# Decoding the fourth token block with the other three in a hybrid SSD, attention and PEER layer

## Chip, cores and metric

One core of one Trainium2 chip runs the whole layer in one launch. The metric is the device time in microseconds of one execution; the figure for the kernel before is the median of three runs. The profile is of one further execution, so its own time stands beside its span below.

## What is computed

512 tokens of width 1024 pass a layer norm, a mixer (16 SSD heads and 8 latent-attention heads, one output projection) and a PEER expert layer. Only the PEER part matters here:

```python
s = einsum('thkd,hknd->thkn', q, sub_keys)          # 8 heads, 2 halves, 128 keys each
sv, si = top_k(s, 16)                               # per half
cand_s = sv[:, :, 0, :, None] + sv[:, :, 1, None, :]
top_s, top_pos = top_k(cand_s.reshape(..., 256), 16)
expert_idx = take_along_axis(cand_i, top_pos)       # one of 16384 experts
gate = softmax(top_s)
act = gelu(x . u_table[expert_idx])                 # 128 experts a token
out = sum(gate * act * v_table[expert_idx])
```

The result then goes through a last residual layer norm.

## The kernel before, in words

**Two ways to do PEER.** The 512 tokens are four blocks of 128. Blocks 0 to 2 (384 tokens) are done densely: the expert tables are cut into 128 chunks of 128 experts, a *U chunk* multiplies one chunk of `u_table` with the tokens (24 matmuls of 336 columns, then GELU on ScalarE, L1416), and a *V chunk* multiplies gated activations with one chunk of `v_table` (18 matmuls of 512 columns, L1680 to L1684). The last 48 tokens of block 2 are left out of the U matmuls and gather their `u_table` rows instead (`ug_fetch`, `ug_dots`). Block 3 is done wholly by gathers: 128 rows a token of `u_table`, then 128 of `v_table` (`gather`, L1540; `fetch`, L1558): POOL issues an indirect DMA of 512 KB for one expert of each of the 128 tokens, and VectorE multiplies (L1572) or accumulates (L1578) it.

**Weights.** Each chunk comes by a 512 KB load on SP's queue (`wir`, L105), is rounded on ScalarE (`wih`, L123), and its low part is made on VectorE (`wil`, L133). Loads, roundings and splits run two chunks ahead of TensorE.

**Order of the work.** Every engine runs its instructions in the order of the program. The order is a plan made by Python generators: a `yield` names the VectorE time that a step is thought to take, and `drive` (L1482) adds half a U chunk to the program whenever the planned TensorE time (3.75 us a chunk, `T_U`) is not ahead of the planned VectorE time. A U chunk charges 1.2 us of VectorE too. The stages from the scores on are:

1. query projection and top 16 of blocks 0 to 3 (`stage1`);
2. `stage2` (L1111): `decode` of blocks 0 to 2, which turns positions into expert numbers by one-hot products (L1093 to L1103) and scores into gates; U chunks between;
3. `build_g` (L1228), the *gate build*: dense gate tiles for blocks 0 to 2 by f16 matmuls, 48 steps. Every fourth step fills a staging tile `stg` of 16 KB a partition, from the pools `gs0` and `gs1` in turn; ScalarE's queue stores it to `gsp` in DRAM in three pieces (L1310), and of the last two staging tiles a small part goes to `gs0` in DRAM (L1306). The last tile (number 11) lies in pool `gs0`. U chunks run between, up to `AHEAD`, later up to `PRE - RES`;
4. `late3` (L1116): block 3's scores and positions, which were parked in DRAM (`t3d`), are loaded again on POOL's queue and decoded alone, beside the U chunks up to number `PRE - 1`;
5. the V stage: `load_g` (L1604) loads gate tiles `gt`, for the first two groups of four chunks on POOL's queue (L1610); `v_prep` (L1630) multiplies activations and gates, `v_hi` and `v_lo` split the product `P` into `Ph` and `Pl`. `GAP` V chunks run alone, then U and V chunks in turn until U's 128 are done, then V alone. Block 3's gathers are spread over the remaining units of work (L1727 to L1731). Each `fetch` keeps four rows in flight.

Activations stay in SBUF for `KEEP` chunks; the next ones are parked in DRAM (`asp`) until the pools `act2` and `act3` open, and come back on POOL's queue (L1411). Of the first chunks (`done`, up to 40) the gates are multiplied in place during the gate build (L1316).

**Pools.** SBUF pools are stacks. `gp2` (rows of the gather, `hd`, `ac`) opens on the right side; in that order on the same side lie `xt`, then `ijp`, then `gs1`, `gs0` and `gb` while the gate build runs. A tile framework adds the waits: the first access in a new pool waits for what the closed pools that it overlaps still have under way, stores included.

The lines of the start of the V stage, in their order:

```python
fill = gather()
next(fill)                       # L1599
...
for q in range(2):
    load_g(q)                    # L1617
refill()
```

Of the kernel before, what the change touches and what calls it, by code (L numbers as in the profile page):

```python
# [11 lines left out]
F32 = mybir.dt.float32  # L12
F32R = mybir.dt.float32r
F16 = mybir.dt.float16
# [21 lines left out]
NA = ND * 32 + 32  # L36
PIECES = 3
FIRST = 40
KEEP = 51
MORE = 12  # L40
REST = 5
LEAD = KEEP + MORE + REST
PRE = 74
AHEAD = 68
GAP = max(0, PRE - LEAD - 1)
UROWS = 4
RES = 3
# [20 lines left out]
def tile_block(ctx: ExitStack, tc: tile.TileContext, I, out):  # L68
# [6 lines left out]
    def pool(name, bufs=1, **kw):  # L75
        p = tc.alloc_tile_pool(name=name, bufs=bufs, **kw)
        opened.append(p)
        return p
# [868 lines left out]
    spare = lambda c0: XT[:, :, c0:c0 + 64].bitcast(F32)  # L947
    wide = lambda z: z.rearrange("p (a b) -> p a b", b=64)
    scl = xt.tile([128, 1], F32, name="scl")
    xt.tile([128, 64], F32, name="edge")  # L950
    one16 = xt.tile([128, NA - NU], F32, name="one16")
    V.memset(one16, 1.0)
# [93 lines left out]
            cand, h = late_c.pop()  # L1046
            yield (0.7 if m == 15 else 0.0) + top16(cand, 88, TS4[:, :, h], PO4[:, :, h])

    t3d = [dram.tile([128, n, 16], dt, name=nm) for n, dt, nm in ((8, F32, "ts3"), (8, U32, "po3"), (16, U32, "ti3"))]

    def decode(p, TS, PO, TI, ia, blocks, nb):
        f4 = lambda z: z.rearrange("p b h k -> p (b h k)")
        g4 = lambda z: z.rearrange("p b h k -> p (b h) k")
        d = p.tile([128, nb, 8, 16], F32, name="dd")
        V.tensor_tensor(g4(d), g4(TS), g4(TS)[:, :, 0:1].to_broadcast([128, nb * 8, 16]), op=OP.subtract)
        sm_ = lambda n, dt=F32: p.tile([128, nb * 128], dt, name=n)
        p3, p2, pf, b1 = sm_("p3", U32), sm_("p2", U32), sm_("pf"), sm_("b1")
        a1, af, sm = p3.bitcast(F32), p2.bitcast(F32), b1[:, :nb * 8]
        abf = p.tile([128, nb, 2, 128], F16, name="abf")
        ti = p.tile([128, 2, 8, 16, 2], F16, name="tif", bufs=min(nb, 2))  # L1060
        pos = f4(PO)
        ab = lambda e: abf[:, :, e]
        v4 = lambda z: z.rearrange("p (b k) -> p b k", b=nb)
        V.tensor_scalar(p3, pos, 3, None, op0=OP.logical_shift_right)
        V.tensor_scalar(p2, pos, 2, None, op0=OP.logical_shift_right)
        V.tensor_copy(pf, pos)
        yield 1.2 if nb > 1 else 0.6
        V.tensor_scalar(a1, p3, -1.0, 0.0, op0=OP.add, op1=OP.max)
        V.scalar_tensor_tensor(af, p2, -6.0, a1, op0=OP.add, op1=OP.max)
        V.tensor_scalar(a1, af, 8.0, 8.0, op0=OP.mult, op1=OP.add)  # L1070
        V.tensor_scalar(b1, af, 4.0, 24.0, op0=OP.mult, op1=OP.add)
        yield 1.3 if nb > 1 else 0.7
        V.tensor_copy(ab(0), v4(af))
        V.tensor_tensor(a1, a1, b1, op=OP.min)
        V.tensor_scalar(b1, af, 0.0, 8.0, op0=OP.is_equal, op1=OP.mult)
        V.tensor_tensor(pf, pf, a1, op=OP.subtract)
        V.tensor_tensor(ab(1), v4(pf), v4(b1), op=OP.add)
        yield 2.0 if nb > 1 else 1.0
        A.activation(f4(d), f4(d), AF.Exp)
        V.tensor_reduce(sm, g4(d), axis=AX.X, op=OP.add)  # L1080
        V.reciprocal(sm, sm)
        for b in range(nb):
            o = IJG[blocks[b]] = (ijp if nb > 1 else p).tile([128, 3, 8, 16], F32, name="ijg", bufs=nb)
            V.tensor_tensor(o[:, 2], d[:, b], sm[:, b * 8:(b + 1) * 8, None].to_broadcast([128, 8, 16]), op=OP.mult)
        yield 1.6 if nb > 1 else 0.8
        sh = [128, 16, 16, 16]
        for b in ((2, 0, 1) if nb > 1 else (0,)):
            for c in range(2):
                A.activation(ti[:, :, :, :, c].rearrange("p e h a -> p h e a"),
                             TI[:, b].rearrange("p (h e) a -> p h e a", e=2), AF.Copy)  # L1090
            eq = p.tile([128, 16, 16, 16], F16, name="eq")
            abv = abf[:, b].rearrange("p e (h k) -> p (e h) k", k=16)
            V.tensor_tensor(eq, abv[:, :, None, :].to_broadcast(sh), ia[:, None].to_broadcast(sh), op=OP.is_equal)  # L1093
            yield 2.3
            eqv = eq.rearrange("p g a (k c) -> p (g a) k c", c=2)
            tv = ti.rearrange("p e h a c -> p (e h a) c")
            V.tensor_tensor(eqv, eqv, tv[:, :, None, :].to_broadcast([128, 256, 8, 2]), op=OP.mult)
            if nb > 1 and b != 1:
                ti = p.tile([128, 2, 8, 16, 2], F16, name="tif", bufs=2)
            yield 2.3  # L1100
            for w in (8, 4, 2):
                V.tensor_tensor(eq[:, :, :w], eq[:, :, :w], eq[:, :, w:2 * w], op=OP.add)
            V.tensor_tensor(IJG[blocks[b]][:, 0:2].rearrange("p e h k -> p (e h) k"), eq[:, :, 0], eq[:, :, 1], op=OP.add)  # L1103
            yield 2.8
            if nb > 1 and b == 2:
                ug_index(p3)
            if nb > 1 and b == 1:
                yield next(UR["dots"])
                g_head(0)

    def stage2():  # L1111
        yield from decode(rt2, TS4[:, :3], PO4[:, :3], TI4[:, :3], iaE, (0, 1, 2), 3)

    late = []

    def late3():  # L1116
        lt = pool("lt", side="right")
        t = [lt.tile([128, 1, n, 16], dt, name=nm) for n, dt, nm in ((8, F32, "ts"), (8, U32, "po"), (16, U32, "ti"))]
        ia = lt.tile([128, 16, 16], F16, name="iaE")
        G.dma_start(ia.rearrange("p a b -> p (a b)"), I["ch"][:, 256:512])  # L1120
        for z, src in zip(t, t3d):
            G.dma_start(z[:, 0], src)
        yield 3.4
        yield from decode(lt, *t, ia, (3,), 1)
        late.append(lt)

    GT, UR = {}, {}
    done = []
# [1 line left out]
    def ug_index(tmp):  # L1130
        ijg = IJG[2]
        f = lambda z: z.rearrange("p h k -> p (h k)")
        ix = tmp[:, :128].bitcast(I32)
        V.scalar_tensor_tensor(ix, f(ijg[:, 0]), 128.0, f(ijg[:, 1]), op0=OP.mult, op1=OP.add)
        G.dma_start(ugi, ix[128 - UG:])
        G.dma_start(ugg, f(ijg[128 - UG:, 2]))
        for k, dst in spread(ugi, UR["ix"]):
            G.dma_start(dst, k)
        G.dma_start(UR["g"], ugg)
        for n in range(UROWS):  # L1140
            ug_fetch(n)
        for dst, t in zip(t3d, (TS4, PO4, TI4)):
            G.dma_start(dst, t[:, 3])
        UR["dots"] = ug_dots()

    def spread(d, t):
# [81 lines left out]
    def build_g():  # L1228
# [44 lines left out]
        for n in range(48):  # L1273
# [24 lines left out]
            if g % 4 == 3:  # L1298
                k = n // 4
                if k < ND:  # L1300
                    done.append(min(FIRST, (un[0] - 2) // 4 * 4))
                    late.append((n + 2, k, stg))
                    e = [done[k] + (128 - done[k]) * x // PIECES for x in range(PIECES + 1)]
                    stores.extend((gsp[k][:, x:y], stg[:, x:y]) for x, y in zip(e, e[1:]))
                else:
                    nc.scalar.dma_start(gs0[:, :, k - ND], stg[:, 0:8].rearrange("j (q i) t -> j q (i t)", q=2))  # L1306
                    e = [8 + 120 * x // PIECES for x in range(PIECES + 1)]
                    stores.extend((gsp[k][:, x:y], stg[:, x:y]) for x, y in zip(e, e[1:]))
# [229 lines left out]
    GS = [-1, 0, 0]  # L1538

    def gather():  # L1540
        yield from late3()
        ijg = IJG.pop(3)
        ix = gp_.tile([128, 128], I32, name="ix")
        f = lambda z: z.rearrange("p h k -> p (h k)")
        V.scalar_tensor_tensor(ix, f(ijg[:, 0]), 128.0, f(ijg[:, 1]), op0=OP.mult, op1=OP.add)
        g3 = gp_.tile([128, 128], F32, name="g3")
        V.tensor_copy(g3, f(ijg[:, 2]))
        close(*late, ijp)
        yield 0.5
        gp2 = pool("gp2", side="right")  # L1550
        x3 = UR["x3"]
        hd = gp2.tile([128, 128], F32, name="hd")
# [5 lines left out]
        def fetch(s):  # L1558
            if s < 256:
                R[s] = gp2.tile([128, D], F32, name="row", bufs=ROWS)  # L1560
                G.indirect_dma_start(out=R[s], out_offset=None, in_=I["u"] if s < 128 else I["v"],  # L1561
                                     in_offset=bass.IndirectOffsetOnAxis(ap=ix[:, s % 128:s % 128 + 1], axis=0))
        for s in range(ROWS - 1):
            fetch(s)
        for s in range(256):
# [26 lines left out]

    aps.append(pool("act3"))
    edge = pool("edge")
    edge.tile([128, 64], F32, name="edge")
    vst = pool("vst")
    gp_ = pool("gp")
    fill = gather()
    next(fill)  # L1599
    gt = {}  # L1600

# [97 lines left out]
    for c in range(2):  # L1699
        while uc < PRE - 1 + c:  # L1700
            u_chunk(uc)
            uc += 1
            if GS[0] < 0:
                pump(fill, 2.6)
        v_hi(c, v_prep(c))
        v_lo()
    more = True
# [175 lines left out]
```

## Time and profile before

| | |
|---|---|
| runs | 1572.33, 1577.47, 1578.97 us (median 1577.47) |
| profiled execution, its own time | 1574.32 us |
| its span | 1572.6 us |
| granted TensorE clock, mean | 0.998 |
| TensorE busy | 1546.8 us (98%) |
| VectorE busy | 1346.1 us (86%) |
| ScalarE busy | 767.9 us (49%) |
| POOL busy | 622.8 us (40%) |
| DMA, mean | 259 GB/s |

Busy shares are means over stages with different limits. A busy TensorE is not TensorE at its peak, since the ends of matmuls are modelled; the times from one matmul's start to the next say more.

### The profile page before, as it was taken

The page shows a single profiled execution, that of the slowest core. Times are in us where ns is not written, and L with a number is a line of the kernel's source. Part 1 is how long each engine was busy: PE and PEld are TensorE (multiplying, and loading weights), DVE is VectorE, ACT ScalarE, POOL GpSimd, SP SyncE. Part 2 cuts the span into 40 slices and gives each one's busy share as a digit, 9 for nine tenths or more (in the row PEclk, how much of TensorE's full clock was granted, in tenths as well). Part 3 has the DMA queues.
Part 4 walks back from the last instruction along what each step waited for, and adds up shares of the span by engine and source line. Part 5 has one row for each costly group of instructions (what it writes and reads, how often), then busy time and mean ns, then how long its engine had stood idle before and what let it go on. Part 6 is the DMA issues. An engine that isn't in the chain of part 4 may idle for free.

```text
span 1572.6 us, 24526 instructions
## 1 busy us (share of the span) xinstructions
PE 1546.8 (98%) x8696; PEld 1358.0 (86%) x8696; DVE 1346.1 (86%) x2643; ACT 767.9 (49%) x1539; POOL 622.8 (40%) x455
## 2 busy tenths in 40 slices
PE   9999999999999999999999999999999999999997
PEld 7887888888888999999998999999988878888886
DVE  8979767747799989999976888888889889899997
ACT  5565467741433547777755444444433344434442
POOL 0010032510134534443114666565555557667610
PEclk9999999999999999999999999999999999999999
DMA  6242122474323568999779999999989999999983
GB/s 253 94 161 83 55 78 54 128 244 148 124 88 101 137 226 291 358 336 326 271 251 335 351 361 358 350 359 386 373 320 371 360 366 372 357 359 364 370 280 141
DMA packets 150171, 406.53 MB, mean 259 GB/s; under 512 B 14280, under 2 KB 55448, under 8 KB 149792
## 3 DMA queue, kind: packets, MB, share of 16 engines
q1 hardware_dynamic: 94080, 208.11, 38.9%
q0 software_dynamic: 50096, 177.12, 31.0%
q10 hardware_dynamic: 5872, 19.73, 3.1%
q8 instruction: 68, 1.11, 0.3%
q14 instruction: 55, 0.45, 0.1%
HBM read 374.16 MB, written 28.65 MB: 256 GB/s over the span
## 4 chain that ended last, share of the span: by engine, by line
PE 75%; DVE 10%; DMA 7%; issue 4%; ACT 3%; POOL 1%; DVEq 0%; ACTq 0%; POOLq 0%
PE va L1684 9%; PE va L1681 9%; PE va L1680 9%; PE pu L86 8%; PE pu L88 8%; PE pu L87 8%; DMA wir<-v 4%; PE pa L87 3%; PE pa L86 3%; PE pa L88 3%; PE pw L87 3%; PE pw L88 3%; PE pw L86 3%; DVE wil L133 2%; DMA wir<-ut 2%
## 5 line engine op out<-in xcount | busy, mean ns | idle before, releaser
L123 ACT ACTIVATE wih<-wir 128x1024 fp32r<-128x1024 f32 (+2 forms) x269 | 277.7, 1033 | 259.4 <-DMA wir<-v 161.2
L133 DVE TENSOR_TENSOR wil<-wir,wih 128x1024 fp32r<-128x1024 f32 (+1 forms) x234 | 282.9, 1212 | 80.5 <-ACT wih L123 55.1
L88 PE MATMUL pu<-XT,wil 128*128 128x336 f32 x1008 | 319.2, 317 | 5.4 <-DVE wil L133 5.3
L1681 PE MATMUL va<-wil,Ph 128*128 128x512 f32 x726 | 283.0, 390 | 0.0
L1561 POOL DMA_INDIRECT row<-v,ix x128 | 217.5, 1699 | 136.6 <-DVE ac L1578 114.7
L1680 PE MATMUL va<-wih,Ph 128*128 128x512 f32 x624 | 243.5, 390 | 0.0
L1561 POOL DMA_INDIRECT row<-u,ix x128 | 186.8, 1460 | 132.6 <-DVE row L1572 96.6
L86 PE MATMUL pu<-XT,wih 128*128 128x336 f32 x648 | 207.5, 320 | 0.0
L87 PE MATMUL pu<-XT,wih 128*128 128x336 f32 x648 | 204.5, 316 | 0.0
L88 PEld LDWEIGHTS pu<-XT,wil 128*128 128x128 f32 x1008 | 189.3, 188 | 8.0 <-DVE wil L133 8.0
L1684 PE MATMUL va<-wih,Pl 128*128 128x512 f32 x624 | 193.2, 391 | 1.4 <-DVE Pl L1671 1.3
L1578 DVE SCALAR_TENSOR_TENSOR ac<-row,hd,ac 128x1024 f32<-128x1024 f32 x128 | 164.1, 1282 | 8.5 <-DMA row<-v,ix 6.8
L1681 PEld LDWEIGHTS va<-wil,Ph 128*128 128x128 f32 x726 | 136.4, 188 | 26.6
L1572 DVE SCALAR_TENSOR_TENSOR row<-row,XT 128x1024 f32<-128x1024 f32 x128 | 150.8, 1222 | 9.7 <-DMA row<-u,ix 9.6
L1684 PEld LDWEIGHTS va<-wih,Pl 128*128 128x128 f32 x624 | 116.9, 188 | 27.3 <-DVE Pl L1671 2.7
L1680 PEld LDWEIGHTS va<-wih,Ph 128*128 128x128 f32 x624 | 117.2, 188 | 22.7
L133 POOL TENSOR_TENSOR wil<-wir,wih 128x1024 fp32r<-128x1024 f32 (+3 forms) x35 | 72.9, 2093 | 154.5 <-PE pw L88 99.4
L87 PEld LDWEIGHTS pu<-XT,wih 128*128 128x128 f32 x648 | 121.9, 188 | 1.1
L86 PEld LDWEIGHTS pu<-XT,wih 128*128 128x128 f32 x648 | 121.7, 188 | 1.2
L1155 POOL DMA_INDIRECT urow<-u,uix x48 | 74.1, 1543 | 107.2 <-DVE urow L1161 98.8
L123 ACT ACTIVATE wihx<-wir 128x1024 fp32r<-128x1024 f32 x67 | 70.9, 1058 | 91.8 <-DMA wir<-ut 55.6
L1663 ACT ACTIVATE Ph<-P 128x384 fp32r<-128x384 f32 x121 | 62.7, 518 | 107.5 <-DVE P L1640 90.2
(520 smaller groups left out, 3389.9 us busy)
## 6 DMA issues: line engine op xcount, KB each, us to landing
wir<-ut SPq DMA_DIRECT2D x128, 512.0 KB, 6.1
wir<-v SPq DMA_DIRECT2D x128, 512.0 KB, 6.7
gt<-gsp SPq DMA_DIRECT2D x22, 768.0 KB, 10.2
wir<-wo SPq DMA_DIRECT2D x26, 512.0 KB, 3.7
wir<-wf SPq DMA_DIRECT2D x18, 512.0 KB, 3.3
wir<-wqr SPq DMA_DIRECT2D x16, 512.0 KB, 3.5
gsp<-stg ACTq DMA_DIRECT2D x12, 464.0 KB, 6.4
de<-acd POOLq DMA_DIRECT2D x8, 512.0 KB, 5.4
```

The costliest lines, as they stand in the source:

```text
L86: T.matmul(ps, lh, rh, start=start, stop=False)
L87: T.matmul(ps, lh, rl, start=False, stop=False)
L88: T.matmul(ps, ll, rh, start=False, stop=stop)
L123: A.activation(h, r, AF.Copy)
L133: self.lo(n).tensor_tensor(l, r, h, op=OP.subtract)
L1155: G.indirect_dma_start(out=UR[n], out_offset=None, in_=I["u"], in_offset=bass.IndirectOffsetOnAxis(ap=UR["ix"][:, n:n + 1], axis=0))
L1561: G.indirect_dma_start(out=R[s], out_offset=None, in_=I["u"] if s < 128 else I["v"], in_offset=bass.IndirectOffsetOnAxis(ap=ix[:, s % 128: ...
L1572: V.scalar_tensor_tensor(wide(r), wide(r), 1.0, x3, op0=OP.mult, op1=OP.mult, accum_out=hd[:, s:s + 1])
L1578: V.scalar_tensor_tensor(ac, r, hd[:, s - 128:s - 127], ac, op0=OP.mult, op1=OP.add)
L1680: T.matmul(va[b][e], Ph[b], h[:, cs], start=c == 0, stop=False)
L1681: T.matmul(va[b][e], Ph[b], l[:, cs], start=False, stop=False)
L1684: T.matmul(va[b][e], Pl[b], h[:, cs], start=False, stop=c == 127)
```

## The change

Block 3 is decoded in `stage2` with the other three, after block 1 and the first gate tile's head; its expert numbers `ix3` and gates `g3` are kept in `xt`. `late3`, the parking in `t3d` and the loads back are gone. `gather()` is advanced twice ahead of the first `load_g`, so that its four first fetches stand there in POOL's program. `PRE` goes from 74 to 72, so V chunk 0 comes after 72 U chunks; `AHEAD` goes from 68 to 70, `KEEP` from 51 to 50, and `GAP`, worked out from them, from 5 to 4. The planner is charged more for the decode. `done` no longer lags two chunks behind.

```diff
-KEEP = 51
+KEEP = 50
...
-PRE = 74
-AHEAD = 68
+PRE = 72
+AHEAD = 70
...
     scl = xt.tile([128, 1], F32, name="scl")
+    ix3 = xt.tile([128, 128], I32, name="ix3")
+    g3 = xt.tile([128, 128], F32, name="g3")
...
-        yield 1.2 if nb > 1 else 0.6
+        yield 1.5
...
-        yield 1.3 if nb > 1 else 0.7
+        yield 1.6
...
-        yield 2.0 if nb > 1 else 1.0
+        yield 2.5
...
-            o = IJG[blocks[b]] = (ijp if nb > 1 else p).tile([128, 3, 8, 16], F32, name="ijg", bufs=nb)
+            o = IJG[blocks[b]] = ijp.tile([128, 3, 8, 16], F32, name="ijg", bufs=3) if b < 3 else p.tile([128, 3, 8, 16], F32, name="ijg3")
...
-        yield 1.6 if nb > 1 else 0.8
+        yield 2.1
...
-        for b in ((2, 0, 1) if nb > 1 else (0,)):
+        for b in (2, 0, 1, 3):
...
-            if nb > 1 and b == 1:
+            if b == 1:
                 yield next(UR["dots"])
                 g_head(0)
+            if b == 3:
+                ijg = IJG.pop(3)
+                f = lambda z: z.rearrange("p h k -> p (h k)")
+                V.scalar_tensor_tensor(ix3, f(ijg[:, 0]), 128.0, f(ijg[:, 1]), op0=OP.mult, op1=OP.add)
+                V.tensor_copy(g3, f(ijg[:, 2]))
+                yield 0.5
 
     def stage2():
-        yield from decode(rt2, TS4[:, :3], PO4[:, :3], TI4[:, :3], iaE, (0, 1, 2), 3)
-
-    late = []
-
-    def late3():
...
+        yield from decode(rt2, TS4, PO4, TI4, iaE, (0, 1, 2, 3), 4)
...
-        for dst, t in zip(t3d, (TS4, PO4, TI4)):
-            G.dma_start(dst, t[:, 3])
         UR["dots"] = ug_dots()
...
-                    done.append(min(FIRST, (un[0] - 2) // 4 * 4))
+                    done.append(min(FIRST, un[0] // 4 * 4))
...
     def gather():
-        yield from late3()
...
-        close(*late, ijp)
-        yield 0.5
+        close(ijp)
         gp2 = pool("gp2", side="right")
...
     edge = pool("edge")
-    edge.tile([128, 64], F32, name="edge")
+    edge.tile([128, 160], F32, name="edge")
     vst = pool("vst")
-    gp_ = pool("gp")
     fill = gather()
+    next(fill)
     next(fill)
...
-            if GS[0] < 0:
-                pump(fill, 2.6)
+            if uc > un[0] + 2:
+                pump(fill, 2.3)
```

## Rows read from the trace of the kernel before

**Rows 1.** The page's part 1: busy us, share of the span, instructions.

```profile
PE 1546.8 (98%) x8696; PEld 1358.0 (86%) x8696; DVE 1346.1 (86%) x2643; ACT 767.9 (49%) x1539; POOL 622.8 (40%) x455
```

**Rows 2.** Stretches: length; busy us of PE, PEld, DVE, ACT, POOL; clock; DMA share; GB/s.

```profile
575.00:800.00 225.00, 220.37 (x1891) 213.65 (x1890) 214.97 (x295) 159.42 (x382) 72.27 (x54) 1.00 0.86 306
800.00:833.00 33.00, 32.75 (x214) 32.47 (x213) 21.43 (x36) 18.27 (x34) 10.16 (x13) 1.00 0.80 271
833.00:1160.00 327.00, 327.00 (x1748) 295.07 (x1747) 276.12 (x449) 142.25 (x290) 191.63 (x134) 1.00 0.98 357
1160.00:1303.00 143.00, 138.59 (x712) 121.28 (x712) 126.47 (x131) 55.00 (x106) 73.88 (x54) 1.00 0.97 356
```

**Rows 3.** Stretch 0 to 799, instructions of L1417 alone: length, ACT busy (count).

```profile
0.00:799.00 799.00, 31.14 (x67) 1.00 0.54 180
```

**Rows 4.** Timeline of DVE, decode of blocks 0 to 2, then of block 3.

```profile
534.20 0.54 DVE L1074 TENSOR_TENSOR p<-p,b 128x384 f32<-128x384 f32 x1
...
536.21 1.22 DVE L133 TENSOR_TENSOR wil<-wir,wih 128x1024 fp32r<-128x1024 f32 x1
...
560.86 2.28 DVE L1093 TENSOR_TENSOR eq<-abf,iaE 128x4096 f16<-128x4096 f16 x1
...
564.20 2.28 DVE L1097 TENSOR_TENSOR eq<-eq,tif 128x4096 f16<-128x4096 f16 x1
...
567.53 2.40 DVE L1102 TENSOR_TENSOR eq<-eq 128x2048 f16<-128x2048 f16 x3
569.97 0.42 DVE L1103 TENSOR_TENSOR ijg<-eq 128x256 f32<-128x256 f16 x1
...
809.65 0.28 DVE L1074 TENSOR_TENSOR p<-p,b 128x128 f32<-128x128 f32 x1
```

**Rows 5.** Timeline of DVE and of PE at the start of the gate build.

```profile
575.18 0.29 DVE L1213 TENSOR_SCALAR unit<-px 128x128 f32<-128x128 f32 x1 [1.37 <-ACT gT L1205]
...
582.30 0.42 PE L88 MATMUL pu<-XT,wil 128*128 128x336 f32 x1 [2.08 <-DVE wil L133]
```

**Rows 6.** Timeline of PE: after the last gate matmul; V chunk 0.

```profile
799.56 0.40 PE L86 MATMUL pu<-XT,wih 128*128 128x336 f32 x1
...
833.30 0.39 PE L1680 MATMUL va<-wih,Ph 128*128 128x512 f32 x1
```

**Rows 7.** Timeline of ACT's queue: the last staging tile's three stores.

```profile
801.00 1.66 ACTq L1310 DMA_DIRECT2D gsp<-stg  x3
```

**Rows 8.** Timeline of POOL, 800 to 832: start, us, [idle before <- releaser].

```profile
800.99 0.57 POOL L1120 DMA_DIRECT2D iaE<-ch  x1 [29.24 <-DMA wir<-ut]
...
812.12 1.08 POOL L1610 DMA_DIRECT2D gt<-gs  x2 [8.94 <-ACT act L1417]
...
824.65 1.95 POOL L1561 DMA_INDIRECT row<-u,ix  x1 [10.37 <-issue]
...
831.14 0.59 POOL L1411 DMA_DIRECT2D acts<-asp  x1 [0.35 <-ACT P L1644]
```

**Rows 9.** DMA issues in 802.2:802.3, 789:795, 831:832: count, KB, us to landing.

```profile
gsp<-stg ACTq DMA_DIRECT2D x1, 640.0 KB, 9.3
...
gsp<-stg ACTq DMA_DIRECT2D x3, 640.0 KB, 6.0
...
acts<-asp POOLq DMA_DIRECT2D x1, 176.0 KB, 8.3
```

**Rows 10.** Landing times of L1610's two loads; of all row gathers.

```profile
DMA to landing us min/median/max: 2.4/2.4/2.4
...
DMA to landing us min/median/max: 5.1/8.1/11.6
```

**Rows 11.** Timeline of ACT: the first V chunk's product.

```profile
830.74 0.22 ACT L1644 ACTIVATE P<-gt 128x32 f32<-128x32 f32 x1
830.99 0.53 ACT L1663 ACTIVATE Ph<-P 128x384 fp32r<-128x384 f32 x1
```

**Rows 12.** Stretch 1567 to 1572, after TensorE's last matmul; columns as in Rows 2.

```profile
1567.00:1572.00 5.00, 0.00 (x0) 0.00 (x0) 2.44 (x7) 0.00 (x0) 0.00 (x0) 0.54 0.27 105
```

More of the change, by code (lines that the diff above doesn't have):

```diff
@@ L1047, in stage1 @@
             yield (0.7 if m == 15 else 0.0) + top16(cand, 88, TS4[:, :, h], PO4[:, :, h])
-    t3d = [dram.tile([128, n, 16], dt, name=nm) for n, dt, nm in ((8, F32, "ts3"), (8, U32, "po3"), (16, U32, "ti3"))]
     def decode(p, TS, PO, TI, ia, blocks, nb):
@@ L1059, in decode @@
         abf = p.tile([128, nb, 2, 128], F16, name="abf")
-        ti = p.tile([128, 2, 8, 16, 2], F16, name="tif", bufs=min(nb, 2))
+        ti = p.tile([128, 2, 8, 16, 2], F16, name="tif", bufs=2)
         pos = f4(PO)
@@ L1097, in decode @@
             V.tensor_tensor(eqv, eqv, tv[:, :, None, :].to_broadcast([128, 256, 8, 2]), op=OP.mult)
-            if nb > 1 and b != 1:
+            if b != 3:
                 ti = p.tile([128, 2, 8, 16, 2], F16, name="tif", bufs=2)
@@ L1104, in decode @@
             yield 2.8
-            if nb > 1 and b == 2:
+            if b == 2:
                 ug_index(p3)
-            if nb > 1 and b == 1:
+            if b == 1:
                 yield next(UR["dots"])
                 g_head(0)
-    def stage2():
-        yield from decode(rt2, TS4[:, :3], PO4[:, :3], TI4[:, :3], iaE, (0, 1, 2), 3)
-    late = []
-    def late3():
[L1117 to L1125, printed above, removed]
+            if b == 3:
[4 more added lines that the diff above has]
+                yield 0.5
+    def stage2():
+        yield from decode(rt2, TS4, PO4, TI4, iaE, (0, 1, 2, 3), 4)
     GT, UR = {}, {}
@@ L1540, in gather @@
     def gather():
-        yield from late3()
[L1542 to L1547, printed above, removed]
-        close(*late, ijp)
-        yield 0.5
+        close(ijp)
         gp2 = pool("gp2", side="right")
@@ L1561, in fetch @@
                 G.indirect_dma_start(out=R[s], out_offset=None, in_=I["u"] if s < 128 else I["v"],
-                                     in_offset=bass.IndirectOffsetOnAxis(ap=ix[:, s % 128:s % 128 + 1], axis=0))
+                                     in_offset=bass.IndirectOffsetOnAxis(ap=ix3[:, s % 128:s % 128 + 1], axis=0))
         for s in range(ROWS - 1):
```

## The prediction

> **What bounds the kernel now.** The page's engine table comes first: TensorE (PE) is busy 1546.8 us, 98% of the span [rows 1]. A share is a mean, so the table by stretches is next: in the gate build PE is busy 220.4 of 225 us, then 32.75 of 33, all of 327 where U and V chunks alternate, and 138.6 of 143 as the U chunks run out [rows 2]. So PE sets the end, and none of its work changes: still 128 U and 128 V chunks, still the same gate matmuls. The time can change only by the gaps between matmuls: 4.6 us in the build, 0.25 behind it, none in the long stretch, 4.4 in the last one. DMA stands at 0.98 there (356 GB/s), so that last 4.4 is a matter of late bytes.
>
> What the reader must keep apart is the *order* and the *cover*. At the build's end 65 U chunks are done (67 instructions on L1417 less two table loads [rows 3]), and nine more, 33.74 us, lie between the last gate matmul and the first V matmul [rows 6]: 3.72 us a chunk, with 0.3 of waiting taken off. These nine now cover the stores of the last staging tile, the late decode, the loads of `gt` and the first four gathers.
>
> I keep the clock of the trace before; after the build everything in fact comes some 14 us later, since U chunks move ahead of it.
>
> **Decode ahead of the build.** The fourth block adds to VectorE's one-hot products 2.28 + 2.28 + 3 x 0.8 + 0.42 = 7.38 us [rows 4]. The 15 elementwise steps grow from 384 to 512 columns; a 128-column step takes 0.28 where a 384-column one takes 0.54 [rows 4], 0.13 more for each 128, so up to 15 x 0.13 = 2 us. With 0.5 for `ix3` and `g3` that is 9.9 us. The planner is charged 9.5, and one U chunk nets 3.75 - 1.2 = 2.55 of cover, so it puts four more U chunks ahead of the build's end: 69 where there were 65, which is also its limit, 72 - 3. PE gets 4 x 3.72 = 14.9 us of work for VectorE's 9.9 + 4 x 1.22 = 14.8 (1.22 is `wil` [rows 4]). Cost 0. Bounds: below nothing is excluded by PE's work; above, what is not covered of one one-hot step, 2.3.
>
> The late decode that goes was about the same 10 us of VectorE, beside nine U chunks where VectorE was busy 21 of 33 us [rows 2]: gain 0. With it go seven small POOL DMAs (three out, four in); POOL was idle behind them [rows 8]: 0.
>
> **Start of the build.** PE waits 2.08 us for `wil` at 582.30, and VectorE had itself waited 1.37 for ScalarE's `gT` at 575.18 [rows 5]. With the other order of decode, block 3's products stand between block 1's gate head and the build, and ScalarE has long finished: -1.3 (bounds -2.1 and 0). The 0.3 behind the build came with the late decode's head: -0.3.
>
> **First V product.** Three U chunks (69, 70, 71) are left ahead of it: it is due at 799.56 + 3 x 3.72 = 810.7 instead of 833.3. Two loads stand before it, and their place on POOL's queue is what matters. The gathers' pool `gp2` holds `hd` 512, `ac` 4096, five rows of 4096 and small tiles of 448 B: 25,536 B a partition. `ijp` (8,576) and `gs1` (16,384) free 24,960, so `gp2` reaches 576 B into `gs0`, where staging tile 11 lies. The first access, `ac` on VectorE and the row gathers on POOL, must therefore wait until that tile's three stores have landed. They are issued from 801.00 on [rows 7]; the third, at 802.22, took 9.3 [rows 9], to 811.5, and POOL, free soon after 803, sits until 812.12 before `gt` [rows 8]: that wait is there already, ending 0.6 us after the landing.
>
> Without block 3's loads beside them, I take the 6.0 us that a store of the tile before took [rows 9]: landed at 808.2. Bounds: 3 x 640 KB at 357 GB/s [rows 2] is 5.5 us from 801.0, 806.5; and 811.5.
>
> Then four gathers: before, from 824.65 to 831.14 less 0.35 idle [rows 8], 6.14 us, so to 814.3. Only behind them does POOL issue the two `gt` loads (before: ahead of the gathers, landing in 2.4 with the queue empty [rows 10]). A load behind four gathers, `acts`, took 8.3 [rows 9]; a row itself takes 5.1 at least, 8.1 at the median [rows 10]. I take 4.2: the least row landing, less 0.9 between the issues, since DMA is at 0.80 here and not at 0.98. Bounds 2.4 and 8.3. The product on VectorE and the 0.22 + 0.53 on ScalarE [rows 11] make 0.9. Sum: 808.2 + 6.1 + 4.2 + 0.9 = 819.4, **8.7 late** (bounds 5.2 and 16.1). VectorE's wait at `ac` also holds `wil` of chunk 71, so part of the gap may show there, inside the 8.7.
>
> The rows show that a load behind gathers lands about as late as they do: 8.3 against 8.1. The Trainium skill, "DMA: Bandwidth & Descriptors", section "Queues, rings and completion order", has it as a rule against such an order: on one DMA engine a completion is signalled only after every earlier write of that engine, across its queues. Read with the median row, 8.1 less 0.9, the lateness would be 11.7 and the whole time about 1589 rather than 1586.
>
> **V chunk 1** finds two dot products and `wil` ahead of its product on VectorE, each about 1.2 [rows 4]; a V chunk covers most: +0.6 (0 to 2.4).
>
> **Clock.** A PE gap of 5 to 9 us may lower the granted clock. It stood at 1.00 in the build stretch that holds the 2.08 gap [rows 2] and at 0.54 in the 5 us after the last matmul [rows 12]. In the long stretch a pair of chunks is 42 of the 1748 matmuls in 327 us [rows 2], 7.86 us, and 3.72 of that is the U chunk: a V chunk takes 4.1 us, and twice that if it ran wholly at the lower level. I take half, +2.0 (0 to 4.1).
>
> **Gathers later on.** With some 13.6 us of U work more ahead of the build's end, less the gaps that go, the first gather begins at 808.2 + 13.6 = 821.8 by the trace's own time, for 824.65 [rows 8]: 3 us sooner. The schedule spreads the rows over `units() - ENDU` at the first dot product: 162 units instead of 160, 1.57 rows a unit for 1.60. That is 0.03 x 512 KB x 2 units = 0.03 MB less for a pair of chunks, 0.08 us at 357 GB/s; over the 16 or so pairs of the last stretch, -1.3 (bounds 0 and -4.4, all of its waits). `KEEP` 50 parks some activations more: 0 (to +0.7). `GAP` 4 for 5 moves a U chunk: 0.
>
> **Sum.** +8.7 + 0.6 + 2.0 - 1.3 - 0.3 - 1.3 = +8.4 on the profiled execution's 1574.32, 1582.7. That execution stands 3.15 under the runs' median, so the median of the changed kernel should be 1582.7 + 3.15 = **1586**.
>
> **Rivals.** *The loads come in time, no change.* If only the tile's overlapping bytes hold the gathers, or the pieces land early, POOL begins at 801 [rows 8]: 801 + 6.1 + 4.2 + 0.9 = 812.2, 1.5 late; without a clock loss +1.5 - 2.9 = -1.4: 1576. Against it: POOL's wait to 812.12 now.
>
> *Faster.* If V chunk 0's `gt` lands before 810.7, nothing new is waited for, and the sparser gathers free all 4.4 of the last stretch and the build another 2: -1.3 - 0.3 - 4.4 - 2.0 = -8: 1569.5. Against it: four gathers ahead of `gt` must fit in 10 us with the stores, and DMA remains at 0.97.
>
> *Much slower.* The stores again land at 811.5, `gt` takes the 8.3 of `acts`, and the clock falls for a whole V chunk: 16.1 + 0.6 + 4.1 - 1.6 = +19.2: 1597. It decides from a PE gap of some 15 us at the first V product. For it: these are the very rows of this place [rows 9]; against: less is loaded beside them.
>
> **How the numbers follow.** Forecast 0.50 (own range 1580 to 1594), no change 0.30, much slower 0.12, faster 0.08. Half a per cent, about what a measurement of this kernel can tell from none, is 7.9 us: from 1569.6 to 1585.4. Of the forecast's half 0.36 lies above that bound and 0.14 inside. So faster 0.08, same 0.30 + 0.14 = 0.44, slower 0.36 + 0.12 = 0.48. The range, 1574 to 1597, leaves out the faster case and the upper half of the much slower one, with a little at the lower edge of no change: under 0.2.
>
> **What would show it.** Right: 69 GELUs on L1417 at the build's end; POOL's first gather only when the last `gsp` store has landed, some 8 us behind the last gate matmul; `gt` landing some 10 us after that; one PE gap of 5 to 10 us before the first va matmul, or shared with `wil` of chunk 71; the gap at the build's start down to 0.8 or less; PE's waits in the last stretch 3 us instead of 4.4. Wrong: a first gather beginning at once behind the build, or `gt` landing within 3 us of issue, or no new PE gap there (then 1570 to 1577); or VectorE holding PE inside the decode, which the planner's four chunks should cover.

## The result, and the profile after

The changed kernel takes 1585.76 us (median of 6 runs, 1584.08 to 1585.99) where the kernel before takes 1577.01 beside it: ratio 1.0057, 95% interval 1.004 to 1.0073. The forecast was 1586, slower. The profiled execution after takes 1585.73 us, its span is 1583.7 against 1572.6. Further down, one execution of `decode_only` (2188.71 us at a mean clock of 0.654) and one of `warm` (2588.48 us at 0.556) ran in a slower state of the chip and are left out of medians and ratios.

First the stretches of the changed kernel (length; busy us of PE, PEld, DVE, ACT, POOL; clock; DMA share; GB/s), cut where its own stages end. They answer to [rows 2].

```profile
575.00:811.00 236.00, 233.75 (x1981) 227.46 (x1980) 225.75 (x306) 165.77 (x392) 79.22 (x60) 1.00 0.88 309
811.00:834.00 23.00, 11.13 (x71) 10.57 (x69) 3.16 (x4) 4.57 (x11) 9.78 (x12) 0.90 0.77 288
834.00:840.00 6.00, 5.95 (x15) 4.70 (x16) 5.32 (x10) 3.65 (x9) 2.87 (x4) 0.53 0.90 269
840.00:1160.00 320.00, 320.00 (x1717) 289.25 (x1716) 268.35 (x429) 140.83 (x283) 190.08 (x129) 1.00 0.96 349
1160.00:1314.00 154.00, 149.16 (x772) 132.42 (x772) 134.96 (x141) 58.55 (x115) 82.00 (x59) 0.99 0.97 356
```

Read the second line: of the 23 us between the gate build and the first V matmul TensorE works 11.1. Elsewhere little has moved: the build idles 2.25 us instead of 4.6, the long stretch not at all, the last one 4.8 instead of 4.4. The third line has the clock: 0.53 in the six us behind the gap.

Who ended these waits stands in the table of waits of PE, 811 to 845 us (line waited for; us in total, times, longest):

```profile
PE va L1663 <- ACT Ph L1646: 9.4, 1, 9.4
PE pu L88 <- DVE wil L133: 2.5, 1, 2.5
```

And the way back from there is the timeline, here lines of POOL, DVE, ACT and PE in order of time (start, us, engine, operation, [idle before <- releaser]):

```profile
810.55 0.22 PE L1284 MATMUL pw<-g,oj 128*128 128x128 f16 x1
...
812.01 2.13 ACTq L1301 DMA_DIRECT2D gsp<-stg  x3
...
819.11 0.69 DVE L1537 TENSOR_SCALAR ac<-XT 128x1024 f32<-128x1024 f32 x1 [11.63 <-ACT aout L1409]
...
819.75 2.08 POOL L1544 DMA_INDIRECT row<-u,ix  x1 [37.00 <-ACT P L1626]
...
820.99 0.42 PE L88 MATMUL pu<-XT,wil 128*128 128x336 f32 x1 [2.51 <-DVE wil L133]
...
825.58 1.19 POOL L1593 DMA_DIRECT2D gt<-gs  x2
...
833.13 0.23 ACT L1627 ACTIVATE P<-gt 128x32 f32<-128x32 f32 x1 [13.97 <-DMA gt<-gs]
...
834.05 0.79 PE L1663 MATMUL va<-wih,Ph 128*128 128x512 f32 x1 [9.41 <-ACT Ph L1646]
```

The last gate matmul is at 810.55. The three stores of staging tile 11 are issued from 812.01; VectorE (`ac`) and POOL (first row) both stand still until 819.11 and 819.75. The releasers named for them are works of ScalarE that ended 0.3 and 0.6 us before, but it is the stores that they wait for: the third, issued at 813.17, took 5.4 us and landed at 818.6, and the experiment `no_overlap` below, where `gp2` no longer reaches tile 11, begins its gathers at 811.59. `gt` is issued at 825.58, behind four gathers, and ScalarE gets it at 833.13. So `gt` took as long as a row:

```profile
gsp<-stg ACTq DMA_DIRECT2D x1, 640.0 KB, 5.4
...
gt<-gs POOLq DMA_DIRECT2D x2, 128.0 KB, 7.4
...
row<-u,ix POOLq DMA_INDIRECT x4, 8.0
```

(DMA issues: count, KB, median us to landing, the store in 813.3 to 813.5, the others between 815 and 830 us; [rows 10] had 2.4 for `gt`.) The GELUs before 812 us are 71, less two table loads 69, which is the forecast's count (length, ACT busy, count; [rows 3] had 67 with the loads):

```profile
0.00:812.00 812.00, 33.41 (x71) 1.00 0.55 182
```

### The profile page after: what moved, and what is told of

It is laid out like the page before. It is cut to its first block, busy times and chain, and to the rows that moved or that the text cites. A ratio compares the mean times of both kernels' runs of the same rounds, so it can differ in the third digit from the quotient of the medians.

```text
span 1583.7 us, 24512 instructions
## 1 busy us (share of the span) xinstructions
PE 1549.5 (98%) x8696; PEld 1361.9 (86%) x8696; DVE 1343.8 (85%) x2620; ACT 766.6 (48%) x1536; POOL 605.3 (38%) x455
## 5 line engine op out<-in xcount | busy, mean ns | idle before, releaser
L86 PE MATMUL pu<-XT,wih 128*128 128x336 f32 x864 | 275.5, 319 | 0.0
L87 PE MATMUL pu<-XT,wih 128*128 128x336 f32 x864 | 272.2, 315 | 0.0
L1544 POOL DMA_INDIRECT row<-v,ix x128 | 192.4, 1503 | 167.7 <-DVE ac L1561 145.1
L1544 POOL DMA_INDIRECT row<-u,ix x128 | 192.5, 1504 | 165.3 <-DVE row L1555 101.9
L1663 PE MATMUL va<-wih,Ph 128*128 128x512 f32 x462 | 182.1, 394 | 9.4 <-ACT Ph L1646 9.4
L87 PEld LDWEIGHTS pu<-XT,wih 128*128 128x128 f32 x864 | 162.5, 188 | 2.2
L86 PEld LDWEIGHTS pu<-XT,wih 128*128 128x128 f32 x864 | 162.2, 188 | 2.3
L1667 PE MATMUL va<-wih,Pl 128*128 128x512 f32 x462 | 144.1, 393 | 3.8 <-DVE Pl L1654 3.8
L1663 PEld LDWEIGHTS va<-wih,Ph 128*128 128x128 f32 x462 | 87.8, 190 | 27.3 <-ACT Ph L1646 9.7
L1667 PEld LDWEIGHTS va<-wih,Pl 128*128 128x128 f32 x462 | 87.5, 190 | 22.7 <-DVE Pl L1654 4.2
```

Of the source, the lines that this page charges most:

```text
L86: T.matmul(ps, lh, rh, start=start, stop=False)
L87: T.matmul(ps, lh, rl, start=False, stop=False)
L1663: T.matmul(va[b][e], Ph[b], h[:, cs], start=c == 0, stop=False)
L1667: T.matmul(va[b][e], Pl[b], h[:, cs], start=False, stop=c == 127)
```

## The experiments

Theory: V chunk 0 waits for a chain on POOL's queue, made of the pool wait for tile 11's stores, four gathers, and `gt` behind them. Rivals: the DMA engines are simply full there; the pool wait is all of it; the decode costs something itself. The table has the median, the ratio to the kernel before in the same set of runs, the time of the one profiled execution, and from this execution the idle time of PE right before the first V matmul (V0) and between 1150 and 1330 us (180 less busy).

| kernel | median us | ratio, 95% interval | profiled us | idle before V0 | idle 1150-1330 |
|---|---|---|---|---|---|
| changed | 1585.76 | 1.0057 (1.004 to 1.0073) | 1585.73 | 9.4 | 4.8 |
| gt_first | 1581.41 | 1.0020 (1.0002 to 1.0038) | 1577.66 | none | 1.9 |
| no_overlap | 1582.14 | 1.0035 (1.0019 to 1.0051) | 1587.81 | 8.3 | 7.5 |
| both | 1578.57 | 1.0010 (0.9994 to 1.0026) | 1576.29 | 3.5 | 3.0 |
| decode_only | 1577.70 | 1.0002 (0.9982 to 1.0021) | 1579.90 | 1.2 | 8.5 |
| gt_first_clear | 1580.47 | 1.0017 (1.0002 to 1.0031) | 1578.08 | 3.2 | 7.1 |
| swap | 1573.94 | 0.9979 (0.9963 to 0.9994) | 1572.44 | 1.4 | 4.1 |
| fewer_rows | 1577.44 | 1.0003 (0.9989 to 1.0018) | 1577.63 | 7.8 | 0.0 |
| warm | 1584.03 | 1.0046 (1.0023 to 1.0068) | 1585.74 | 2.0 | 4.1 |
| two_first | 1582.68 | 1.0044 (1.0025 to 1.0062) | 1583.58 | 5.6 | 5.1 |
| cover | 1587.39 | 1.0079 (1.0059 to 1.0098) | 1583.47 | 9.3 | 3.4 |
| cover_no_dots | 1580.08 | 1.0011 (0.9991 to 1.0032) | 1582.59 | 1.3 | 9.7 |
| swap44 | 1574.66 | 0.9975 (0.9956 to 0.9995) | 1575.92 | 1.0 | 6.3 |

The last column is of one execution each, and it partly tells executions apart instead of kernels: of the five whose profiled execution lies over 1 us below the median, four idle 1.9 to 4.1 us there (gt_first_clear 7.1); of the five over 1 us above it, four idle 6.3 to 9.7 (warm 4.1).

**gt_first: the two `gt` loads ahead of the gathers.**

```diff
     fill = gather()
     next(fill)
-    next(fill)
...
     for q in range(2):
         load_g(q)
+    next(fill)
```

> The changed kernel with the two gt loads issued ahead of the four first row gathers; nothing else moves. Theory (order on POOL's queue): gt is issued when tile 11's stores have landed, some 8 us behind the last gate matmul, and lands within 3 us, so the 9.6 us PE gap before V chunk 0 goes and with it the 2.5 us of lower clock; the 2.7 us wait for wil of chunk 71 stays, since ac on VectorE still waits for the same stores. 12.1 us less: about 1574. Rival (bytes): gt is late because the DMA engines are full there, whatever the order: gt takes 7 us to land again, V chunk 0 is 6 us late or more, about 1581 or above.

Measured: 1581.41, less than half of the gain that was expected (the profiled execution, 1577.66, is one of the quicker ones). The theory's first half holds. Lines of the timelines of POOL, ScalarE, VectorE and PE of gt_first:

```profile
820.08 1.14 POOL L1592 DMA_DIRECT2D gt<-gs  x2 [36.90 <-ACT P L1626]
...
822.64 0.23 ACT L1627 ACTIVATE P<-gt 128x32 f32<-128x32 f32 x1 [2.71 <-DMA gt<-gs]
...
832.31 1.22 DVE L1555 SCALAR_TENSOR_TENSOR row<-row,XT 128x1024 f32<-128x1024 f32 x1 [2.86 <-DMA row<-u,ix]
833.46 0.08 DVE L1555 DVE_READ_ACCUMULATOR row<-row,XT 128x1 f32 x1
833.46 0.18 DVE L1623 TENSOR_TENSOR P<-acts,gt 128x32 f32<-128x32 f32 x1
...
834.32 0.50 PE L1663 MATMUL va<-wih,Ph 128*128 128x512 f32 x1 [3.54 <-ACT Ph L1646]
```

`gt` lands in 2.4 us again and V chunk 0 starts as soon as U chunk 71 is done, 826.5. But the rows are now later, and the two dot products that the program puts ahead of V chunk 1's product wait for them on VectorE: PE waits 3.5 us there. The wait has moved one chunk on. The wait for `wil` of chunk 71 also stays, 2.8 us.

**no_overlap: `gp2` clear of the staging tile.**

```diff
-        hd = gp2.tile([128, 128], F32, name="hd")
+        hd = gp_.tile([128, 128], F32, name="hd")
...
-        mv, rs = norm_stats(gp2, ac, "lg")
+        mv, rs = norm_stats(gp_, ac, "lg")
...
+    gp_ = pool("gp")
```

> The changed kernel with hd and the small norm tiles in a pool of their own on the left side, so that gp2 no longer reaches into gs0; the four gathers still stand ahead of gt. Theory: ac and the gathers begin at the end of the gate build, 8 us sooner; no wait for wil of chunk 71; gt is still held until tile 11's stores have landed (its own pool overlaps gs0 too), then lands about 5 us later, behind rows already under way: V chunk 0 some 2.5 us late instead of 12.3, the clock holds: about 1573.5. Rival (the pool wait is all of it): V chunk 0 not late at all, 1571. Rival (bytes): gathers beside the stores delay those and gt, V chunk 0 8 us late or more, 1581 or above.

Measured: 1582.14, V chunk 0 8.3 us late. The gathers do begin at 811.6 and the wait for `wil` is gone, but the theory's number fell and the rival on bytes got its 8. POOL's timeline of no_overlap:

```profile
811.59 2.04 POOL L1544 DMA_INDIRECT row<-u,ix  x1 [28.88 <-ACT stg L1286]
...
823.96 1.17 POOL L1594 DMA_DIRECT2D gt<-gs  x2 [6.57 <-DMA asp<-aout]
```

And its DMA issues from 811 to 835 us (count, KB each, median us to landing):

```profile
gsp<-stg ACTq DMA_DIRECT2D x3, 640.0 KB, 6.8
...
gt<-gs POOLq DMA_DIRECT2D x2, 128.0 KB, 5.2
...
row<-u,ix POOLq DMA_INDIRECT x6, 11.4
```

Beside the gathers, and a weight load issued at 812.77, the stores take 6.8 us instead of 4.2 (medians of three), so the pool of `gt` (which overlaps the same tile) is free 4 us later than in the changed kernel, where POOL went on at 819.75. `gt` then lands at 829.2, when ScalarE takes it. Two megabytes of rows and two of stores are under way together here.

**both: the two edits together.**

> Both edits: gt ahead of the gathers, and gp2 clear of gs0. Theory: the waits at ac and at gt's place in the queue are both gone; gt lands 10 to 11 us behind the last gate matmul, when V chunk 0 is due, so the gap is under 1 us and the clock stays at 1.00: 1585.8 - 12.3 - 2.5 = 1571, below the kernel before. Rival (bytes): no better than either edit alone, 1581 or above. Rival (the decode costs what the order does not): 1575 to 1577, with new PE waits in the decode or the gate build.

Measured: 1578.57, V chunk 0 3.5 us late. `gt` again lands in 2.4, but is issued at 823.08, 11.3 us behind the last gate matmul where gt_first has 9.1: with `wil` no longer held, two weight loads (issued at 814.12 and 817.81, in gt_first only from 821.73 on) run beside the stores, which take 5.9 us for 4.2. A wait removed let in traffic that lengthened the next wait.

**decode_only: the early decode with the old start of the V stage** (PRE 74, AHEAD 68, gt first, gathers behind; KEEP stays 50).

```diff
-PRE = 72
-AHEAD = 70
+PRE = 74
+AHEAD = 68
...
     next(fill)
-    next(fill)
...
-            if uc > un[0] + 2:
-                pump(fill, 2.3)
+            if GS[0] < 0:
+                pump(fill, 2.6)
```

> The decode of all four blocks ahead of the gate build, with the V stage's start as before: PRE 74, AHEAD 68, gt first, gathers from the second U chunk behind it on (KEEP stays at 50, for the room). Theory: the decode is covered by four more U chunks and saves the 2.4 us wait at the start of the build and the 0.4 behind it; five U chunks lie before V chunk 0, 18.6 us, so no wait there beyond 1 us: 1577.0 - 2.8 = 1574. Rival (the decode ahead costs PE time): 1580 or more with PE waits between 530 and 590 us. Rival (the V stage wants PRE 72): slower than the version with both edits by over 3 us.

Measured: 1577.70, not to be told from the kernel before. No new waits in decode or build (PE is busy all 45 us from 530 to 575, and idles 2.25 us in the build as in the changed kernel), so the decode ahead costs nothing that shows; V chunk 0 hardly waits. This run clears the decode of the loss: it belongs to the start of the V stage. What the build gained is not seen in the time: PE idles 8.5 us in the last U stretch of the profiled execution.

**gt_first_clear and swap: the remaining waits one by one.** gt_first_clear also moves `ac` behind the 64th row and takes the two dot products out of V chunk 1's way. swap is gt_first_clear with one line more, so that tile 11 lies in `gs1`, which the pool of `gt` doesn't touch. Both have the lines of gt_first too; the last hunk is swap's alone.

```diff
-        V.tensor_scalar(wide(ac), x3, ALPHA, None, op0=OP.mult)
...
+            if s == 64:
+                V.tensor_scalar(wide(ac), x3, ALPHA, None, op0=OP.mult)
...
-            if uc > un[0] + 2:
-                pump(fill, 2.3)
...
-                stg = gs[(n // 4 + 1) % 2].tile([128, 128, 32], F32, name="stg")
+                stg = gs[n // 4 % 2].tile([128, 128, 32], F32, name="stg")
```

> gt ahead of the gathers as in gt_first, and two more waits taken out: ac's first write moves from the V stage's start to the 64th row, and no dot products are put ahead of V chunk 1's product. Theory: wil of chunk 71 no longer waits, so weight loads run beside the stores as in both, these land some 4 us later and V chunk 0 is 3 to 4 us late; V chunk 1 does not wait (1.1 us in both, 3.7 in gt_first). 1578.6 - 1.5 - some clock = 1576. Rival (what is won at V chunk 0 comes back as waits in the last U stretch, since the DMA engines bound all of it from there on): 1579 or more, with over 8 us of PE waits between 1150 and 1330 us. Rival (the DVE wait was harmless): as gt_first, 1581.

> As gt_first_clear, and the staging tiles take the two pools in the other turn, so that the last one lies in gs1 and the pool of gt, P, Ph and Pl (which overlaps gs0 alone) waits for the tile before it. Theory: gt then needs only the small store of the last tile to gs0 in DRAM, issued first and landed 2.1 us after; gt is issued some 4 to 5 us behind the last gate matmul instead of 9 to 12 and V chunk 0 is on time, gap under 1 us; clock 1.00: 1573. Rival (weights or U chunks late by the same traffic): V chunk 0 still 3 us late, for wil of chunk 71 or of V chunk 0: 1577. Rival (given back in the last stretch): 1578 or more.

Measured: 1580.47 and 1573.94. In gt_first_clear V chunk 0 is 3.2 us late and chunk 1 not at all, as expected, but the time is that of its rivals (1579 or more, 1581), and the last stretch idles 7.1, where one of them wanted over 8. swap is the version that beats both kernels: 0.9979, interval 0.9963 to 0.9994. Lines of the timelines of POOL and PE of swap:

```profile
817.15 1.10 POOL L1593 DMA_DIRECT2D gt<-gs  x2 [34.02 <-DMA gsp<-stg]
...
822.80 1.01 POOL L1543 DMA_INDIRECT row<-u,ix  x1 [4.55 <-DMA asp<-aout]
...
823.60 0.50 PE L1664 MATMUL va<-wih,Ph 128*128 128x512 f32 x1 [1.37 <-ACT Ph L1647]
```

And its stretch 811 to 845 (columns as in the first fence, whose second and third line have 17.1 us of PE in 29):

```profile
811.00:845.00 34.00, 32.63 (x177) 29.32 (x175) 17.08 (x28) 17.11 (x38) 15.71 (x19) 1.00 0.92 332
```

`gt` is issued at 817.15, 6.2 us behind the last gate matmul, while the stores are still under way (their queue takes 99% of the DMA engines' time from 818 to 819 us, 18% from 820 to 821). It takes longer beside them: ScalarE, which waits for it, has it 5.4 us after its issue. The gathers come behind it, V chunk 0 waits 1.4 us and the clock stays at 1.00. Of the 6.5 us between the two medians the traces tie 1.8 to the gap and about 1.6 to the clock, an estimate from eight matmuls 0.43 us apart behind the gap of gt_first_clear where 0.23 is usual, and none in swap. The other 3 lie in the last stretch and are not shown to come from this edit.

**fewer_rows: the last 32 gathers of `v_table` left out** (with their share of the sum over experts).

```diff
-            if s < 256:
+            if s < 224:
...
-        for s in range(256):
+        for s in range(224):
...
-            want = 253 - max(0.0, (256 - GS[2]) * (left - ENDU) / GS[1])
+            want = 221 - max(0.0, (224 - GS[2]) * (left - ENDU) / GS[1])
```

> The changed kernel with the last 32 of block 3's 128 v_table gathers and accumulations left out, and the rows that are left spread over the same units. It leaves out part of the sum over experts. Theory (the waits of the last U stretch come from row gathers that saturate the DMA engines): DMA share there falls under 0.95 and PE's waits between 1150 and 1330 us go from 7 to under 2 us: 1585.8 - 5.5 = 1580; the wait at V chunk 0 stays, 12 us. Rival (they come from the order on VectorE, not from bytes): the waits stay at 5 us or more, 1584 or above.

Measured: 1577.44, 3 us below the expectation. The last stretch has no idle time at all, while the gap at V chunk 0 stays. Its stretches (columns as in the first fence):

```profile
845.00:1150.00 305.00, 305.00 (x1639) 275.95 (x1639) 239.14 (x381) 133.03 (x268) 153.31 (x106) 1.00 0.92 323
1150.00:1330.00 180.00, 180.00 (x931) 159.82 (x930) 154.62 (x187) 73.47 (x141) 92.41 (x63) 1.00 0.98 351
```

How the rows hold TensorE there is in the changed kernel's trace: the waits of VectorE between 1150 and 1330 us, then lines of the timelines of VectorE and PE.

```profile
DVE ac L1561 <- DMA row<-v,ix: 9.3, 7, 2.4
...
1298.26 1.28 DVE L1561 SCALAR_TENSOR_TENSOR ac<-row,hd,ac 128x1024 f32<-128x1024 f32 x1 [2.14 <-DMA row<-v,ix]
1299.46 0.55 DVE L1654 TENSOR_TENSOR Pl<-P,Ph 128x384 fp32r<-128x384 f32 x1
...
1300.07 0.93 PE L1667 MATMUL va<-wih,Pl 128*128 128x512 f32 x2 [3.76 <-DVE Pl L1654]
```

`Pl` stands behind accumulations that wait for their rows, 9.3 us in all; in fewer_rows VectorE waits for no row there. So the waits come with the rows. Whether the bytes make them is not shown: the run takes out VectorE's 1.28 us for each row too, and the share of the DMA engines stayed at 0.98, where the theory wanted it under 0.95. (The waits in the changed kernel's trace are 4.8 us, not the 7 of the expectation.) Its ten runs also lie within 2.3 us (1576.6 to 1578.9), where the 35 of the kernel before beside them spread over 12; but the changed kernel's six, with all rows, lie within 1.9, so where the scatter comes from stays open.

**warm: matmuls inside the gap.**

```diff
+    def warm(n):
+        for i in range(n):
+            T.matmul(va[0][i % 2][:, :NU], XTH[:, i % 8, :128], XTH[:, i % 8, :NU], start=True, stop=True)
...
         v_lo()
+        if c == 1:
+            warm(56)
```

> The changed kernel with 56 more matmuls of 336 columns, whose result is overwritten, between U chunk 71 and V chunk 0, where TensorE waits for 9.6 us: about 8.6 us of work inside the gap. Theory: the granted clock stays at 1.00 behind the gap, and the 2.5 us that V chunk 0 loses at the lower level come back: 1583.3. Rival (the clock falls for the 2.7 us wait at chunk 71 or for another reason): no gain or more time, 1585.8 or above.

Measured: 1584.03, with an interval that overlaps the changed kernel's, so the time shows no gain. Here ScalarE got `gt` 1.2 us later against the end of the build, so 2.0 us of idle time were left. The clock fell all the same: seven matmuls from 837.5 on ran at the lower level (0.57 between 837 and 841 us), where the changed kernel has twelve. What a gap filled in full gives back was not shown.

**two_first: two gathers ahead of `gt`, two behind.**

```diff
         for s in range(ROWS - 1):
             fetch(s)
+            if s == 1:
+                yield 0.1
...
         load_g(q)
+    next(fill)
```

> The changed kernel with two row gathers ahead of the gt loads instead of four, the other two behind them. Theory (the lateness of gt grows with the gathers ahead of it): gt is issued 2.5 us sooner than the 825.6 of the changed kernel and lands in about 5 us, between the 2.4 of none ahead and the 7.4 of four; V chunk 0 starts 5 us sooner, at about 829: 1585.8 - 5 = 1581. Rival (the rows' bytes count, not the number ahead): gt lands no sooner than 831, 1584 or above. Rival (V chunk 1's two dot products give it back, since rows 2 and 3 are later): V chunk 1 waits 3 us or more, 1584.

Measured: 1582.68, 1.7 above the expectation. `gt` was issued at 824.48 and its two loads took 7.5 us, no less than behind four gathers (7.4). The first landed at 832.2, no sooner than 831, as the rival on bytes had it, though the time stays under that rival's 1584. The time from issue to landing does not grow with the number ahead, as the theory had it: two are enough to make it as late as a row (7.6 here). V chunk 0 still waits less, 5.6 us for 9.4, since `gt` is issued 2.1 us sooner against the end of the build.

**cover and cover_no_dots: four more U chunks ahead of V chunk 0.**

```diff
-PRE = 72
+PRE = 76
```

cover_no_dots also takes out the two lines `if uc > un[0] + 2: pump(fill, 2.3)` between the U chunks.

> The changed kernel with PRE 76 instead of 72 (and GAP 8, which follows from it): four more U chunks stand between the gate build and V chunk 0, the order on POOL's queue stays. Theory (V chunk 0 waits because only three U chunks cover stores, gathers and gt, some 23.5 us of work): seven chunks cover 26 us, the 9.6 us gap goes and the clock stays at 1.00; the 2.7 us for wil of chunk 71 stays; four more activations are parked, 1.4 MB more of traffic: 1585.8 - 12 + 1 = 1575. Rival (the transfers stretch with the time there is): still 5 us late or more, 1580 or above. Rival (more comes back in the last U stretch): PE waits between 1150 and 1330 us over 9 us, 1578 or above.

> As cover, without the dot products that the loop there put between the U chunks and so ahead of V chunk 0's product on VectorE; the row gathers and gt keep the changed kernel's order. Theory (in cover gt had landed by 839.4 and the product stood behind dot products that waited for rows 2 and 3 until 849): V chunk 0 starts at about 839, with under 2 us of gap, clock 1.00: 1587.4 - 9.4 - 2.0 - 1.5 (wil of a later chunk behind the same dots) = 1574.5. Rival (gt behind four gathers is late whatever the cover): V chunk 0 waits 4 us or more, 1580. Rival (four more parked activations cost what the cover wins): no wait at V chunk 0, yet over 9 us between 1150 and 1330 us, 1579.

Measured: 1587.39 and 1580.08. cover missed by 12 us, for a reason of its own: `gt` was there by 839.4, but the loop between the U chunks had put six dot products ahead of the product, and the last two waited for the fifth and sixth row, issued at 838.06 and 840.29 (the expectation of cover_no_dots calls them rows 2 and 3). Lines of the timelines of VectorE and PE of cover:

```profile
847.80 1.23 DVE L1555 SCALAR_TENSOR_TENSOR row<-row,XT 128x1024 f32<-128x1024 f32 x1 [1.83 <-DMA row<-u,ix]
...
848.95 0.19 DVE L1623 TENSOR_TENSOR P<-acts,gt 128x32 f32<-128x32 f32 x1
...
849.80 0.79 PE L1663 MATMUL va<-wih,Ph 128*128 128x512 f32 x1 [9.25 <-ACT Ph L1646]
```

Without them (cover_no_dots) V chunk 0 starts at 840.0 after 1.3 us of waiting, at full clock, as expected. Enough cover cures the order at V chunk 0. But PE then idles 9.7 us in the last stretch and the time is that of the third case, 1580; whether the parked activations cause that, as this rival says, no run shows.

**swap44: fewer bytes in the gates.**

```diff
-FIRST = 40
+FIRST = 44
```

> swap with FIRST 44 instead of 40: four more activations have their gates multiplied in place for six of the ten staging tiles, so 0.4 MB less is stored and 0.4 MB less loaded, the latter among the V chunks 40 to 43 at the beginning of the stretch with waits; VectorE has 0.8 us more in the gate build and 1.4 us less there. Theory (bytes set the waits between 1150 and 1330 us): 0.4 MB at 365 GB/s, 1 us less: 1573, which can't be told from swap by time; the waits there 6 us for 7. Rival (the gate build gets longer by VectorE's work): 1575, new waits between 700 and 810 us.

Measured: 1574.66, not to be told from swap. Its profiled execution shows no less idle time in the last stretch (6.3, swap 4.1), so the theory on bytes is not borne out at 0.4 MB.

## Why the prediction was right, and where it was not

The mechanism was the forecast's, and so was the sign: PE's work did not change, the decode cost nothing under four more U chunks, and one new gap before V chunk 0 outweighed the rest. By its steps, from the profiled executions:

| step | forecast us | measured us |
|---|---|---|
| build, start and rest | -1.3 | -2.4 (idle 4.6 to 2.25) |
| behind the build | -0.3 | -0.25 |
| last store landed, after the last gate matmul | 8.6 | 8.0 (818.6) |
| from there to the first gather | 0 | 1.2 (819.75) |
| four gathers | 6.1 | 5.8 (819.75 to 825.58) |
| `gt` from issue to landing | 4.2 | 7.4 |
| product to V chunk 0 | 0.9 | 0.9 |
| gap before V chunk 0, all | +8.7 | +11.9 (2.5 + 9.4) |
| V chunk 1 | +0.6 | 0 |
| clock behind the gap | +2.0 | +2.4 (12 matmuls, 0.43 apart for 0.23) |
| last U stretch | -1.3 | +0.4 (idle 4.4 to 4.8) |
| clock there, behind the 3.8 us wait at 1300 | 0 | +1.6 (eight matmuls; 0.57 from 1300 to 1304) |

The steps that add up (build, behind it, gap, V chunk 1, clock, last stretch) come to 13.7 as measured, where the spans differ by 11.1. Another 1.1 went the other way ahead of 531 us (PE idle 8.0 to 6.9); no row singles out the rest.

**The term that was mis-sized is `gt`'s landing.** "I take 4.2: the least row landing, less 0.9 between the issues, since DMA is at 0.80 here" was the choice that failed. The row at the same place in the queue (`acts`, 8.3 [rows 9]) was the better witness. With 2.4 for none ahead, 7.5 for two and 7.4 for four, `gt` lands when the rows ahead of it do. The landings say the same: the first `gt` lands at 833.1 behind a fourth row at 832.7 in the changed kernel, at 832.2 behind a second row at 831.6 in two_first, and at 829.2 behind a fourth row at 828.9 in no_overlap. The Trainium skill, "DMA: Bandwidth & Descriptors", section "Queues, rings and completion order", has that as a rule (on one DMA engine a completion is signalled only after every earlier write of that engine); the forecast, reading the rows by it, had 7.2 as the other choice, and the traces agree.

**The rest of the agreement is partly luck.** The forecast for the profiled execution was 1582.7, and it took 1585.73. The step that added 3.15 us, because the profiled execution of before lay under its median, did not hold after: median 1585.76. The two errors cancel. The 8.6 us to the waiters is luck too: 6.0 for the last store was the median of the three of the tile before, the last of the three took 5.4, and the 0.5 us from its landing to `ac` (1.2 to the first gather) stood at nothing.

**The last stretch was forecast the wrong way.** Rows 0.03 sparser a unit did not lower its waits. fewer_rows shows that they come with the rows. What decides their size in a whole kernel is open: they range from 1.9 to 9.7 us over kernels with the same rows, the executions of one kernel differ by several us, and each kernel has one profile only. That a gain at V chunk 0 comes back there fits decode_only, gt_first_clear and cover_no_dots (7.1 to 9.7), but not gt_first, both and swap, which gain it too and idle 1.9 to 4.1, nor no_overlap (late at V chunk 0, and 7.5).

Of the rivals, "the loads come in time" failed at its condition: the gathers did wait for the stores. "Much slower" needed the last store at 9.3 again; it took 5.4, issued 2.6 us behind the last gate matmul as before (813.17 - 810.55, for 802.22 - 799.56). The gap of some 15 us that it wanted was 11.9; but its price for the load, 8.3, was nearer to the 7.4 measured than the 4.2 taken. "Faster" failed at its condition, `gt` in time for V chunk 0; swap, which nearly meets it, shows that such a kernel exists, at 3 us.

Of the signs that were named, 69 GELUs, a first gather only behind the stores, one gap of 5 to 10 us shared with `wil`, and the gap at the build's start came as said. `gt` landed 13.4 us behind the first gather's start instead of some 10, and the waits of the last stretch did not fall to 3.

## What to carry to other kernels

When a step is moved ahead in the program, list what stands behind it on its queue: the loads that the next stage needs first belong ahead of transfers that only need to be early. A freed buffer is not free while its stores run, and which buffer the last tile lies in is a free choice; one index here went with 6.5 us (swap against gt_first_clear), of which the traces explain about half. And a wait taken out starts transfers: look at what these slow down before counting the gain.

## What was not expected of the hardware

A 128 KB load behind two row gathers took 7.5 us, behind four 7.4, with none ahead 2.4, and with stores still under way some 5.4 (swap). Stores of 640 KB took 4.2 us with little beside them, 5.9 beside weight loads and 6.8 beside row gathers and a weight load (medians of three).

The length of a gap alone did not tell what the granted clock would do. Behind the same 2.5 us gap at chunk 71 it stayed at 1.00 in the changed kernel (820.9 to 824.3 us) and stood at 0.50 in fewer_rows (821.4 to 824.7), in which twelve matmuls went 0.28 us apart where 0.15 is usual. Behind warm's 2.0 us gap it fell, 1.5 us after TensorE had gone on; behind swap's 1.4 us gap it did not. The changed kernel's 9.4 us gap was followed by 0.53.
